# The convolution's layernorm moved behind the fifth head, its projection behind the seventh, and eight of its taps made diagonal matmuls

## The chip, the cores and the metric

One core of one Trainium2 chip runs the whole program. The metric is the device time of one execution in microseconds (us), as the median of several runs. A profile of one execution stands beside it; its times count from the start of its span.

## The reference

The program is two transformer blocks over 512 tokens of width 1024. The change lies in the mixer of the first block, where half of the width is attention and half is a gated convolution:

```python
q, k = rope(rmsnorm(q)), rope(rmsnorm(k))      # 8 heads of 64, 2 key/value heads
attn_out = softmax(q @ k.T) @ v
h = a * sigmoid(gate)                          # 512 channels
h = depthwise_conv(h, conv_dw)                 # 31 taps over time, one weight per channel and tap
h = silu(layernorm(h + conv_b))                # over the 512 channels
x = x + concat([attn_out, h]) @ w_out
```

Behind it come a product-key mixture of experts (128 candidates per token out of 16384 experts) and the whole second block (an RWKV-7 time mix, a sparse attention, a feed-forward), which the change doesn't touch.

## The kernel before

Everything is held transposed: channels on the 128 partitions, the 512 tokens along the free axis, so the 512 convolution channels are four blocks of 128x512. All of the change is in `phase1`, which fills the first 267 us. Large products are three fp32r matmuls each (`mm3`, lines 265 to 267: high by high, low by high, high by low); weights stream through `Stream.next`, which splits each 128x1024 tile on ScalarE (L246) and GpSimd (L248). Products that are given fp32 operands directly, such as the rotation of `head_norm_rope` (L381) or the channel sums (L491), appear in the trace as two matmul records per instruction.

`conv_in` makes one channel block's gated input `hp` (padded to 542 columns) and does the first five taps on ScalarE and GpSimd (`side`). `taps` is a generator: for each block it takes a PSUM bank of the tag `po`, writes tap 5 into it with one VectorE instruction (L353), adds taps 6 to 30 with one VectorE instruction each (L355, 25 of them), and adds `side` into `acc[j]` (L357). `advance(n)` draws n steps of it. Each head's `scores` writes four score tiles into the four banks of the tag `pb`, takes the row maxima (L437, L438), exponentiates into tiles `pr` (L440) and scales them on GpSimd (L442); `values` transposes them (L454, into `pb` banks), splits the result (L282, L283) and multiplies with V (L456 to L458) into a `po` bank that a pair of heads shares. `conv_norm` sums `acc` over channels (L491), squares (L497), takes the row statistics (L928, L934, L935), spreads them (L963), scales (L503), applies silu (L504) and splits (`mch`, `mcl`). `project` multiplies that by half of w_out into x (96 matmuls of 512 columns); `last` does the attention's half.

The loop over heads, with the lines around it:

```python
scores(0); advance(TAPS); conv_in()            # TAPS = 12
for s in range(8):
    if s == 0: query()
    if s < 7: scores(s + 1)
    advance(TAPS)
    values(s)
    if s == 0: conv_in()
    if s in (1, 2): query()
    if s == 3:
        advance(200)                           # all steps that are left
        cs = conv_norm()
    if s == 5:
        project(cs)
```

A planner orders the instructions: it goes through the program with estimated times, and each engine gets the earliest instruction in program order that is ready. Each engine then executes its list strictly in that order. Tiles of one tag share a fixed number of buffers (`po` 2, `mm` 2, `pb` 4, the work tiles `c2` 21, the weight tiles `c4` 12). The tiles `pr`, the splits of `values`, the squares of `conv_norm` and its eight result tiles are all `c2`.

Of the kernel before, what the change touches and what calls it, by code (L numbers as in the profile page):

```python
# [14 lines left out]
OP = mybir.AluOpType  # L15
# [3 lines left out]
P = 128  # L19
S = 512  # L20
# [201 lines left out]
class Stream:  # L222
# [30 lines left out]
    def next(self):  # L253
        self.do_split(self.i + 1 + self.ahead)
        r = self.split.pop(self.i)
        self.i += 1
        return r
# [21 lines left out]
def split_plain(c, x, name, shape=None):  # L279
    nc = c.nc  # L280
    h, lo = c.t2(name + "h", F32R), c.t2(name + "l", F32R)
    nc.scalar.copy(h, x)  # L282
    nc.vector.tensor_sub(lo, x, h)  # L283
    return h, lo
# [11 lines left out]
def phase1(c, st):  # L296
    nc = c.nc
    ident, ones, bones, rot = (c.sq[:, i, :] for i in range(4))
# [19 lines left out]
    def proj(tag="mm"):  # L318
        ps = c.bank(tag, 2)
        mm3(nc, ps, st.next(), xs, kall)  # L320
        return ps
# [3 lines left out]
    def conv_in():  # L325

        j = len(conv)
        a, g = c.t2("ca"), c.t2("cg")
        tag = "mm" if conv else "po"
        nc.vector.tensor_mul(a, proj(tag), rs)  # L330
        nc.vector.tensor_mul(g, proj(tag), rs)
        nc.scalar.activation(g, g, AF.Sigmoid)
        hp = c.sm("hp", [P, S + 30], bufs=4)
        nc.gpsimd.memset(hp[:, 0:15], 0.0)
        nc.gpsimd.memset(hp[:, S + 15:], 0.0)
        nc.vector.tensor_mul(hp[:, 15:15 + S], a, g)
        conv.append(hp)
        w, side = c.vec("cdw", j * 31, 31), c.sm("side", [P, S], bufs=4)
        nc.scalar.activation(side, hp[:, 0:S], AF.Identity, scale=w[:, 0:1], bias=c.vec("cb", j))
        for tap in range(1, SIDE):  # L340
            t = c.sm("tap", [P, S], bufs=2)
            nc.scalar.activation(t, hp[:, tap:tap + S], AF.Copy, scale=w[:, tap:tap + 1])
            nc.gpsimd.tensor_add(side, side, t)
        sides.append(side)
# [3 lines left out]
    def taps():  # L348

        for j in range(4):  # L350

            w, hp, ps = c.vec("cdw", j * 31, 31), conv[j], c.bank("po", 2)
            nc.vector.tensor_scalar(ps, hp[:, SIDE:SIDE + S], w[:, SIDE:SIDE + 1], None, op0=OP.mult)  # L353
            for tap in range(SIDE + 1, 31):
                nc.vector.scalar_tensor_tensor(ps, hp[:, tap:tap + S], w[:, tap:tap + 1], ps, op0=OP.mult, op1=OP.add)  # L355
                yield
            nc.vector.tensor_add(acc[j], ps, sides[j])  # L357
            yield

    tp = taps()  # L360

    def advance(n):
        for _ in range(n):
            next(tp, None)

    def head_norm_rope(p, g):

        t, sq = c.t2("hn"), c.t2("hsq")
        nc.scalar.activation(t, p, AF.Copy, scale=g)
        nc.scalar.activation(sq, p, AF.Square)  # L370
        pn = c.bank()
        for n in range(4):
            nc.tensor.matmul(pn[:, n * 2:n * 2 + 2], sq[:, n * P:(n + 1) * P], bones[:, 0:P:64], start=True, stop=True)
        r = c.sm("hr", [P, 4, 2], bufs=5)

        nc.vector.scalar_tensor_tensor(r, pn[:, 0:8].rearrange("p (n h) -> p n h", n=4), 1.0 / 64,
                                       e2[:, :, None].to_broadcast([P, 4, 2]), op0=OP.mult, op1=OP.add)
        rf = r.rearrange("p n h -> p (n h)")
        nc.gpsimd.tensor_tensor(rf, rf, c.mhalf, op=OP.pow)
        pr = c.bank()  # L380
        nc.tensor.matmul(pr, rot, t, start=True, stop=True)  # L381
        u = c.t2("hu")
        nc.vector.tensor_mul(u, pr, c.rope[:, 1, :])
        nc.gpsimd.tensor_mul(t, t, c.rope[:, 0, :])
        nc.vector.tensor_add(t, t, u)
        return t, r

    conv_in()
    t, r = head_norm_rope(proj(), c.vec("kg"))
    rb = c.t2("rb")  # L390
    nc.scalar.copy(rb.rearrange("p (n v) -> p n v", n=8), r.rearrange("p n h -> p (n h)")[:, :, None].to_broadcast([P, 8, 64]))
    ps = c.bank()
# [6 lines left out]
    def query():  # L399
        t, r = head_norm_rope(proj(), qg)  # L400
        qs.append(split_plain(c, t, "hs") + (r,))
# [9 lines left out]
    for kv in range(2):  # L411
        s = slice(kv * 64, kv * 64 + 64)
# [12 lines left out]
    def scores(s):  # L425
        j, kv = divmod(s, 2)
        rows = slice(kv * 64, kv * 64 + 64)
        qh, ql, r = qs[j]
        prob[s] = []
        for qi in range(4):  # L430
            sl = slice(qi * P, (qi + 1) * P)
            sc = c.bank()
            nc.tensor.matmul(sc, qh[rows, sl], kh[rows, :], start=True, stop=False)
            nc.tensor.matmul(sc, qh[rows, sl], kl[rows, :], start=False, stop=False)
            nc.tensor.matmul(sc, ql[rows, sl], kh[rows, :], start=False, stop=True)
            m, z = c.sm("mx", [P, 1]), c.sm("zs", [P, 1])
            nc.vector.tensor_reduce(m, sc, axis=AX.X, op=OP.max, negate=True)  # L437
            nc.vector.tensor_mul(m, m, r[:, qi, kv:kv + 1])  # L438
            pr = c.t2("pr")
            nc.scalar.activation(pr, sc, AF.Exp, scale=r[:, qi, kv:kv + 1], bias=m, accum_out=z)  # L440
            nc.vector.reciprocal(z, z)
            nc.gpsimd.tensor_mul(pr, pr, z.to_broadcast([P, S]))  # L442
            prob[s].append(pr)
# [22 lines left out]
    def project(xs):  # L466

        for j in range(KD):
            if j % 2 == 0:
                w = st.next()  # L470
            ps = c.bank("mm", 2)
            mm3(nc, ps, w, xs, range(4), off=j % 2 * 4)
            nc.vector.tensor_add(x[j], x[j], ps)
# [12 lines left out]
    def conv_norm():  # L486

        cv = acc
        pm = c.bank("mm", 2)
        for j in range(4):  # L490
            nc.tensor.matmul(pm, ones, cv[j], start=j == 0, stop=j == 3)  # L491

        def csquares():
            for j in range(4):
                nc.vector.scalar_tensor_tensor(cv[j], pm, -1.0 / 512, cv[j], op0=OP.mult, op1=OP.add)
                sq = c.t2("csq")
                nc.scalar.activation(sq, cv[j], AF.Square)  # L497
                yield sq

        cr = spread_rows(c, rstd_rows(c, csquares(), 1.0 / 512, EPS, 4, tag="mm"), tag="mm")  # L500
        ch, cl = [], []
        for j in range(4):
            nc.vector.tensor_mul(cv[j], cv[j], cr)  # L503
            nc.scalar.activation(cv[j], cv[j], AF.Silu, scale=c.vec("clg", j), bias=c.vec("clb", j))  # L504
            h, lo = split_plain(c, cv[j], "mc")
            ch.append(h)
            cl.append(lo)
        return ch, cl

    scores(0)  # L510
    advance(TAPS)
    conv_in()
    for s in range(8):
        if s == 0:
            query()
        if s < 7:
            scores(s + 1)
        advance(TAPS)
        values(s)
        if s == 0:  # L520
            conv_in()
        if s in (1, 2):
            query()
        if s == 3:
            advance(200)
            cs = conv_norm()
        if s == 5:
            project(cs)
    return last


HALVES = [slice(0, 256), slice(256, 512)]
SIDE = 5
TAPS = 12


# [381 lines left out]
def rstd_rows(c, sqs, scale, eps, count=KD, mean=None, tag="pb"):  # L918

    nc = c.nc
    ones = c.sq[:, 1, :]
    ps = c.bank(tag, 4 if tag == "pb" else 2)
    n = 0
    for sq in sqs:
        for i in range(4):
            nc.tensor.matmul(ps[:, i:i + 1], sq[:, i * P:(i + 1) * P], ones[:, 0:1],  # L928
                             start=n == 0 and i == 0, stop=n == count - 1 and i == 3)
        n += 1  # L930
    c.n += 1
    r = c.sb.tile([P, 4], F32, name=f"rr_{c.n}", tag="rr", bufs=4)
    mean = r if mean is None else mean
    nc.vector.tensor_scalar(mean, ps[:, 0:4], scale, eps, op0=OP.mult, op1=OP.add)  # L934
    nc.gpsimd.tensor_tensor(r, mean, c.mhalf[:, 0:4], op=OP.pow)  # L935
    return r
# [21 lines left out]
def spread_rows(c, r, dst=None, tag="pb"):  # L958

    nc = c.nc  # L960
    ps = c.bank(tag, 4 if tag == "pb" else 2)
    for i in range(4):
        nc.tensor.transpose(ps[:, i * P:(i + 1) * P], r[:, i:i + 1].to_broadcast([P, P]), c.sq[:, 0, :])  # L963
    if dst is None:
        return ps
    nc.scalar.copy(dst, ps)
    return dst
# [1157 lines left out]
```

## Time and profile before

| | us |
|---|---|
| median of 3 runs | 2903.32 |
| lowest, highest | 2900.66, 2912.34 |
| the profiled execution | 2895.1 |
| its span | 2893.3 |
| `phase1`, up to the last matmul of the heads | about 267 |

The profile lists engines as PE (TensorE matmul), PEld (its weight loads), DVE (VectorE), ACT (ScalarE), POOL (GpSimd) and SP (the queue of most DMAs). A row of the timeline is start, duration, engine, line, operation, output <- inputs, count, and in brackets the idle time before it with what ended it. Matmul records overlap: what one costs is read from the start of one to the start of the next. In a view by stretches each engine's busy time stands with its number of instructions, and then the granted TensorE clock as a share of full speed (0.50 is 1.2 GHz, 1.00 is 2.4 GHz).

### The profile page before, as it was taken

The numbers are of one execution on the slowest core, as the hardware profiler recorded it, in microseconds if no ns is written. First come the engines' busy times: TensorE is split into PE (matmuls) and PEld (weight loads), VectorE is DVE, ScalarE is ACT, GpSimd is POOL, SyncE is SP. The second block draws the span as 40 slices with busy tenths as digits, with TensorE's granted clock in tenths as the row PEclk, the third lists the DMA queues.
The fourth block names the chain that finished last, engine by engine and source line by source line (L and its number), as shares of the span: only waits on it lengthen the run. The fifth ranks groups of instructions, "written<-read, shape, count | busy, mean of one in ns | idle before, by whom it ended". The sixth has DMA issues, their size and how long they took to land.

```text
span 2893.3 us, 42190 instructions
## 1 busy us (share of the span) xinstructions
PE 2752.7 (95%) x15555; PEld 2357.6 (81%) x15555; DVE 2070.6 (72%) x3972; ACT 1222.8 (42%) x2104; POOL 1199.6 (41%) x959
## 2 busy tenths in 40 slices
PE   8959999999899999999999998999989989999998
PEld 6638899999788888888888777888877768888887
DVE  7585899988788888888885469685438865477721
ACT  5624334677333333333335542112337753444431
POOL 5713350000433333333334676433457736544444
PEclk9969999999999999999999999989989999999999
DMA  4101235688999999999975764645632236233332
GB/s 145 51 0 50 84 115 179 209 289 297 367 351 343 339 339 340 348 343 334 346 261 147 225 171 135 211 130 177 197 116 75 66 130 214 78 98 95 94 96 73
DMA packets 270915, 553.99 MB, mean 191 GB/s; under 512 B 41394, under 2 KB 147890, under 8 KB 268916
## 3 DMA queue, kind: packets, MB, share of 16 engines
q1 hardware_dynamic: 219264, 370.91, 39.7%
q0 software_dynamic: 36864, 134.23, 12.9%
q10 hardware_dynamic: 14580, 46.15, 4.4%
q8 instruction: 122, 2.00, 0.3%
q14 instruction: 85, 0.70, 0.1%
HBM read 464.77 MB, written 83.89 MB: 190 GB/s over the span
## 4 chain that ended last, share of the span: by engine, by line
PE 59%; DVE 8%; DMA 3%; POOL 2%; issue 1%; SPq 1%; ACT 0%; POOLq 0%; ACTq 0%; DVEq 0%
PE pb L858 11%; PE mm L265 8%; PE mm L267 8%; PE mm L266 8%; PE po L858 6%; PE pb L265 2%; PE pb L266 2%; PE pb L267 2%; DVE c4y L1547 1%; PE pb L1634 1%; DVE prob L1969 1%; PE pb L1646 1%; PE mm L1995 1%; DVE ptl L1998 1%; DMA kz<-nk_d 1%
## 5 line engine op out<-in xcount | busy, mean ns | idle before, releaser
L248 POOL TENSOR_TENSOR wl<-wr,wh 128x1024 fp32r<-128x1024 f32 x203 | 504.0, 2485 | 416.4 <-ACT wh L246 151.5
L246 ACT CAST wh<-wr 128x1024 fp32r<-128x1024 f32 x319 | 334.7, 1050 | 496.7 <-PE mm L266 150.6
L690 POOL DMA_INDIRECT ur<-in_u,eix x128 | 150.2, 1174 | 586.6 <-DVE og L786 182.6
L683 ACT CAST vh<-vr 128x512 fp32r<-128x512 f32 x256 | 146.0, 619 | 138.8 <-PE pb L858 138.7
L690 POOL DMA_INDIRECT vr<-in_vrow,eix x128 | 147.8, 1155 | 98.8 <-DVE acc L816 28.2
L684 DVE TENSOR_TENSOR vl<-vr,vh 128x512 fp32r<-128x512 f32 x256 | 167.2, 687 | 23.7 <-ACT vh L683 23.1
L248 DVE TENSOR_TENSOR wl<-wr,wh 128x1024 fp32r<-128x1024 f32 x116 | 142.0, 1224 | 51.6 <-ACT wh L246 50.0
L816 DVE SCALAR_TENSOR_TENSOR acc<-vr,hc,acc 128x1024 f32<-128x1024 f32 x128 | 163.6, 1278 | 0.0
L858 PE MATMUL pb<-vh,ah 128*128 128x512 f32 x512 | 159.7, 393 | 0.0
L858 PE MATMUL pb<-vl,ah 128*128 128x512 f32 x512 | 158.4, 390 | 0.0
L858 PE MATMUL pb<-vh,al 128*128 128x512 f32 x512 | 157.1, 391 | 0.0
L808 DVE CUSTOM_DVE_ANT_0 ur<-ur,hnt 128x1024 f32<-128x1024 f32 x128 | 155.6, 1218 | 0.0
L858 PEld LDWEIGHTS pb<-vl,ah 128*128 128x128 f32 x512 | 96.1, 188 | 21.9
L858 PEld LDWEIGHTS pb<-vh,ah 128*128 128x128 f32 x512 | 96.1, 188 | 20.8
L858 PEld LDWEIGHTS pb<-vh,al 128*128 128x128 f32 x512 | 96.2, 188 | 20.4
L794 ACT ACTIVATE wb<-pb 128x512 f32<-128x512 f32 x96 | 98.9, 1160 | 26.8 <-PE pb L791 25.2
L833 ACT ACTIVATE mm<-mm 128x384 f32<-128x384 f32 x60 | 28.5, 475 | 190.7 <-PE mm L267 190.7
L1976 POOL TENSOR_TENSOR prob<-prob,nz 128x128 f32<-128x128 f32 (+3 forms) x128 | 88.7, 725 | 38.5 <-DVE nz L1973 26.2
L1192 DVE TENSOR_TENSOR tot<-tot,sq 128x512 f32<-128x512 f32 x11 | 17.1, 1551 | 112.0 <-ACT sq L1189 112.0
L858 PE MATMUL po<-vh,ah 128*128 128x512 f32 x256 | 80.2, 394 | 3.2 <-ACT ah L837 3.2
L835 DVE TENSOR_TENSOR mm<-mm,wt 128x384 f32<-128x384 f32 x60 | 33.8, 564 | 67.0 <-ACT mm L833 66.8
L858 PE MATMUL po<-vh,al 128*128 128x512 f32 x256 | 79.8, 391 | 0.1
(1408 smaller groups left out, 8646.9 us busy)
## 6 DMA issues: line engine op xcount, KB each, us to landing
wr<-in_ws SPq DMA_DIRECT2D x191, 512.0 KB, 3.6
wr<-in_uT SPq DMA_DIRECT2D x128, 512.0 KB, 4.9
vr<-in_vrow SPq DMA_DIRECT2D x128, 512.0 KB, 6.7
w_d<-wb ACTq DMA_DIRECT2D x12, 2048.0 KB, 7.5
wt<-w_d SPq DMA_DIRECT2D x32, 768.0 KB, 9.4
gh_d<-gh ACTq DMA_DIRECT2D x68, 192.0 KB, 3.9
gh<-gh_d SPq DMA_DIRECT2D x68, 192.0 KB, 7.6
rd_d<-z SPq DMA_DIRECT2D x24, 256.0 KB, 3.1
```

The source lines that it names most:

```text
L246: c.nc.scalar.copy(h, r)
L248: eng.tensor_sub(lo, r, h)
L265: nc.tensor.matmul(ps, w[0][:, sl], xs[0][k], start=first and a == 0, stop=False)
L266: nc.tensor.matmul(ps, w[0][:, sl], xs[1][k], start=False, stop=False)
L267: nc.tensor.matmul(ps, w[1][:, sl], xs[0][k], start=False, stop=last and a == n - 1)
L683: nc.scalar.copy(h[:, s], r[:, s])
L684: nc.vector.tensor_sub(lo[:, s], r[:, s], h[:, s])
L690: nc.gpsimd.indirect_dma_start(out=t, out_offset=None, in_=src, in_offset=bass.IndirectOffsetOnAxis(ap=eix[:, s:s + 1], axis=0))
L794: nc.scalar.activation(wb[:, :, t4:t4 + 4].rearrange("p e t -> p t e"), wp.rearrange("p (t e) -> p t e", t=4), AF.Copy, scale=1.0 / GSCALE)
L808: nc.vector.tensor_tensor_reduce(out=u, in0=u, in1=hnt, scale=1.0, scalar=0.0, op0=OP.mult, op1=OP.add, accum_out=hc[:, s:s + 1])
L816: nc.vector.scalar_tensor_tensor(acc, v, ghs[gi][:, s:s + 1], acc, op0=OP.mult, op1=OP.add)
L858: nc.tensor.matmul(outs[i][half], ps[a][:, ts], vs[v][:, half * 512:(half + 1) * 512], start=et == 0 and n == 0, stop=et == NE - 1 and n == 2)
```

## The change

Taps 5 to 12 of each block are no longer VectorE instructions. GpSimd builds a tile `dg` of eight 128x128 diagonal matrices (the identity times the tap's weights), and eight fp32 matmuls of 512 columns accumulate these taps into the `po` bank; the whole of this is one step of the generator. VectorE goes on with taps 13 to 30. A block is thus 20 steps rather than 26. `conv_norm` is called at s == 4, behind `values(4)`, and `project` at s == 6, behind `values(6)`; `advance(200)` stays at s == 3.

```diff
-            nc.vector.tensor_scalar(ps, hp[:, SIDE:SIDE + S], w[:, SIDE:SIDE + 1], None, op0=OP.mult)
-            for tap in range(SIDE + 1, 31):
+
+            dg = c.t4("dg").rearrange("p (a b) -> p a b", a=NPE)
+            nc.gpsimd.tensor_tensor(dg, ident[:, None, :].to_broadcast([P, NPE, P]),
+                                    w[:, SIDE:SIDE + NPE, None].to_broadcast([P, NPE, P]), op=OP.mult)
+            for t in range(NPE):
+                nc.tensor.matmul(ps, dg[:, t, :], hp[:, SIDE + t:SIDE + t + S], start=t == 0, stop=t == NPE - 1)
+            yield
+            for tap in range(SIDE + NPE, 31):
                 nc.vector.scalar_tensor_tensor(ps, hp[:, tap:tap + S], w[:, tap:tap + 1], ps, op0=OP.mult, op1=OP.add)
                 yield
             nc.vector.tensor_add(acc[j], ps, sides[j])
...
         if s == 3:
             advance(200)
+        if s == 4:
             cs = conv_norm()
-        if s == 5:
+        if s == 6:
             project(cs)
...
 SIDE = 5
+NPE = 8
 TAPS = 12
```

## Rows read from the trace of the kernel before

**Rows 1.** The page, busy time, share of the span and instructions of TensorE.

```profile
PE 2752.7 (95%) x15555; PEld 2357.6 (81%) x15555; DVE 2070.6 (72%) x3972; ACT 1222.8 (42%) x2104; POOL 1199.6 (41%) x959
```

**Rows 2.** Busy times by stretches; after POOL the granted clock, DMA share, GB/s.

```profile
50.00:105.00 55.00, 53.23 (x216) 40.29 (x216) 27.69 (x53) 27.11 (x44) 38.44 (x25) 0.94 0.20 59
105.00:166.00 61.00, 55.44 (x232) 36.97 (x232) 55.70 (x114) 34.03 (x66) 32.41 (x27) 0.94 0.08 25
166.00:212.00 46.00, 12.34 (x41) 8.71 (x41) 34.63 (x55) 5.82 (x9) 1.01 (x1) 0.50 0.00 0
212.00:267.00 55.00, 54.15 (x250) 40.98 (x250) 27.17 (x57) 27.73 (x52) 21.73 (x16) 0.95 0.13 39
```

**Rows 3.** Timeline of TensorE, 165 to 222 us.

```profile
165.25 0.39 PE L435 MATMUL pb<-hsh,hsl 64*128 64x512 f32 x1
183.51 2.08 PE L491 MATMUL mm<-acc,sqm 128*128 128x512 f32 x2 [17.87 <-DVE acc L357]
195.98 2.07 PE L491 MATMUL mm<-acc,sqm 128*128 128x512 f32 x2 [10.39 <-DVE acc L357]
...
211.91 1.22 PE L265 MATMUL mm<-mch,wh 128*128 128x512 f32 x2 [2.91 <-ACT mch L282]
...
220.15 1.91 PE L454 MATMUL pb<-sqm,pr 128*128 128x128 f32 x16
```

**Rows 4.** Timeline of ScalarE, 198 to 217 us.

```profile
198.87 2.36 ACT L497 ACTIVATE csq<-acc 128x512 f32<-128x512 f32 x4 [33.50 <-DVE acc L495]
...
213.19 1.64 ACT L282 CAST mch<-acc 128x512 fp32r<-128x512 f32 x3
...
216.14 0.78 ACT L440 ACTIVATE pr<-pb,mx,hr 128x512 f32<-128x512 f32 x1
```

**Rows 5.** Timeline of VectorE, 67 to 196 us.

```profile
67.03 0.69 DVE L357 TENSOR_TENSOR acc<-po,side 128x512 f32<-128x512 f32 x1
...
108.43 0.75 DVE L353 TENSOR_SCALAR po<-hp,vecs 128x512 f32<-128x512 f32 x1
...
146.87 0.69 DVE L357 TENSOR_TENSOR acc<-po,side 128x512 f32<-128x512 f32 x1
...
168.88 0.75 DVE L353 TENSOR_SCALAR po<-hp,vecs 128x512 f32<-128x512 f32 x1
169.54 0.15 DVE L438 TENSOR_TENSOR mx<-mx,hr 128x1 f32<-128x1 f32 x1
169.60 13.26 DVE L355 SCALAR_TENSOR_TENSOR po<-hp,vecs,po 128x512 f32<-128x512 f32 x20
...
195.24 0.69 DVE L357 TENSOR_TENSOR acc<-po,side 128x512 f32<-128x512 f32 x1
```

**Rows 6.** Timeline of TensorE at 107 us: the first matmul of values(0).

```profile
107.85 0.50 PE L456 MATMUL po<-pth,avh 128*128 128x512 f32 x1
```

**Rows 7.** Groups of instructions, 25 to 267 us: busy us, mean ns, idle before.

```profile
L355 DVE SCALAR_TENSOR_TENSOR po<-hp,vecs,po 128x512 f32<-128x512 f32 x100 | 73.3, 751 | 1.2
L248 POOL TENSOR_TENSOR wl<-wr,wh 128x1024 fp32r<-128x1024 f32 x18 | 44.0, 2448 | 32.6 <-issue 15.4 <-PE mm L266 10.2 <-ACT wh L246 3.6
L442 POOL TENSOR_TENSOR pr<-pr,zs 128x512 f32<-128x512 f32 x32 | 32.6, 1043 | 38.5 <-DVE zs L441 21.9 <-DVE mx L438 16.5
```

**Rows 8.** Timeline of TensorE, 131 to 133 us: an fp32 matmul among fp32r ones.

```profile
131.44 1.10 PE L381 MATMUL pb<-hn,sqm 128*128 128x512 f32 x2
132.47 0.49 PE L433 MATMUL pb<-hsh,hsh 64*128 64x512 f32 x1
132.81 0.39 PE L434 MATMUL pb<-hsl,hsh 64*128 64x512 f32 x1
133.04 0.39 PE L435 MATMUL pb<-hsh,hsl 64*128 64x512 f32 x1
```

**Rows 9.** Timelines of VectorE and GpSimd at 45 us, side by side.

```profile
45.27 1.28 POOL L343 TENSOR_TENSOR side<-side,tap 128x512 f32<-128x512 f32 x1
45.35 1.75 DVE L385 TENSOR_TENSOR hn<-hn,hu 128x512 f32<-128x512 f32 x1
```

## The prediction, made before the change was run

> **What bounds the kernel now.** The first view is the page's busy table: TensorE is busy for 95% of the span [rows 1], so time can be gained only where it waits, or lost by giving it work. The second is the busy time by stretches [rows 2]. In `phase1` TensorE is full from 50 to 105 us (53.23 of 55), nearly so from 105 to 166 (55.44 of 61) and from 212 to 267 (54.15 of 55), but from 166 to 212 it is busy for 12.34 of 46, at a granted clock of 0.50; there VectorE is busiest, with 34.63. The timeline of TensorE says for what it waits [rows 3]: after the last score matmul at 165.25 it stands idle for 17.87 and then 10.39 us, each time for an `acc` (L357), which is the end of a block's taps. VectorE's timeline shows these taps running with little between them from 168.88 to 195.24 [rows 5].
>
> The third question is why the heads stop meanwhile. The maxima of head 5 were done at 169.54 [rows 5], yet its first exponential ran at 216.14, behind `csq` at 198.87 and `mch` at 213.19 [rows 4]; ScalarE had been idle 33.50 us. All of these take `c2` tiles, and their order is the program's (`conv_norm` stands ahead of scores(5)). I read it as buffers of one tag being handed out in program order. The `po` banks say the same: block 0 was complete at 67.03, but block 1 began at 108.43, right behind the first matmul of values(0) at 107.85, whose bank comes before it in the program [rows 5, 6].
>
> **The moved norm.** With `conv_norm` behind values(4), head 5's exponentials and head 4's values no longer stand behind it. They fill the wait with the transposes (1.91 us [rows 3]), 12 matmuls of 512 columns at 0.23 (start to start [rows 8]), 2.8, and the twelve of scores(6), 2.8: 7.5 us of TensorE that now run behind 212. Head 6's exponentials then stand behind `mch` as head 5's did, so TensorE runs dry again after these. `project` is filler in either place, 96 matmuls of 0.23 or 22 us; one step later it competes less with values(5) and scores(7), and I cost that at nothing as the stretch from 212 on is full. Its weights stay in `c4` one step longer, and `last`'s are loaded behind them; GpSimd and ScalarE are half idle there [rows 2], and if that cover failed a weight tile's split would cost 2.45 [rows 7].
>
> **The taps on TensorE.** VectorE loses 32 instructions: 0.663 each where they run in a row (13.26 over 20 [rows 5]), 0.751 as the mean of records [rows 7], so 21 to 24 us. Block 0's quarter of it ran beside a full TensorE and is worth nothing.
>
> TensorE gains 32 fp32 matmuls of 512 columns. The fp32 matmul of L381 starts at 131.44 and the next one at 132.47 [rows 8], 1.03 us; the next record is 0.10 longer than its like, so at least 0.93 is the engine's own. I take 0.95, near the row, 30 us in sum. The bounds: 0.46, if two records followed each other as fp32r ones do (15 us in all), and 1.04 (2.08 at half clock halved [rows 3], 33 us); a block's eight at half clock would be 16.6 rather than 7.6.
>
> GpSimd builds `dg` four times, 1024 columns each: 2.1 from the scaling by a broadcast factor (2 x 1.043) to 2.45 from the subtraction of two full tiles [rows 7], 8 to 10 us in all, on an engine that is half idle. On the path lies only the last one, and only if it is built late; I take 0, at most 2.5. Its `c4` buffer is one of 12 for the time of eight matmuls; I take that as free, since the weights are split two tiles ahead, and bound it by one split, 2.45.
>
> An addition of two SBUF tiles on VectorE took 1.75 us beside GpSimd's at 45.27 [rows 9], while one with a PSUM operand takes 0.69 [rows 5]: up to 1.1 lost for a collision. The Trainium skill (SBUF — State Buffer, section SBUF: two separate sides) has a rule for this that speaks against the new GpSimd work: VectorE with two SBUF inputs and GpSimd hold their common port pair for a whole instruction, and the other blocks. By it four more tiles cost VectorE up to 10 us, by the row 4.4; the taps read PSUM and one SBUF tile and would escape, so neither changes my sum by more than a microsecond.
>
> **The sum, from place to place.** Blocks 0 and 1 need only their gated inputs and, being 20 steps long, both stand ahead of values(0) now. Their 16 matmuls (15.2) meet a TensorE with 1.8 idle in 55 us and push everything by 15. VectorE, 27.69 busy of 55 there, takes their other taps at no cost. Blocks 2 and 3 (15.2) fall into what was 105 to 166, where 5.6 us are idle; I let them fill 4, and push by 11. So the scores of head 5 end near 165.6 + 15 + 11 = 192.
>
> Block 3 needs a `po` bank, which it gets when block 2 is complete and values(2) has begun. Counting block 2's matmuls to about 160 and its 18 taps among the heads' work to about 175, block 3's matmuls share TensorE with values(3) and end near 187. Then 18 taps at 0.66 to 0.75 and some 3 us of head 4's subtractions give the last `acc` at about 202. From the end of the last `acc` (195.93) to the first matmul of `project` (211.91) took 16.0 [rows 3, 5]; some of it at half clock, so 13 to 16 now, and `project` starts at 216. Of the 55 us behind it (212 to 267), 7.5 have moved ahead and some 2.5 of half-clock matmuls at its start are kept as they are: 47.5, and `phase1` ends at 263 to 264 rather than 267. That is 3 to 4 us; a count by TensorE alone gives the frame: before, 33.7 idle in 166 to 212, 6 lost to the clock there and 7.4 idle in 50 to 166, 47 in all; after, 30 more work, 10 to 12 idle at the norm's chain, some 2 lost to the clock and 2 to 4 idle before it, 44 to 48: between -1 and 3. I take 4, because VectorE, at 55.70 of 61 before, no longer delays the heads' steps, which neither count includes. The rest of the program depends on x and is TensorE-bound, so that it moves by the same.
>
> The profiled execution took 2895.1 (span 2893.3 and 1.8 around it), 8.2 below the median of 2903.3. It would become 2891, and the median 2899.
>
> **The rivals.** *The wait vanishes altogether* (faster): the planner places block 3's matmuls before values(3), so that the last `acc` is there when the heads are, near 190. For it speaks VectorE's freed 21 us; against it that block 3 needs block 2's bank. The gain is 47 - 30 = 17, and with matmuls of 0.85 20: 2883 to 2886. Chance 0.2.
>
> *The diagonal matmuls come last* (slower): block 3's eight go behind scores(5), as the planner prefers earlier program lines and TensorE has a backlog of 26 us by then. Place: between the last `acc` and the first `mch` matmul. 192 + 7.6 + 18 x 0.75 + 3 + 16 = 232, and 47.5 behind it: 279.5, 12 us later, 2916. It decides from a last `acc` later than about 204 (204 + 16 + 47.5 = 267.5). For it speaks that TensorE has no room from 50 to 166; against it the latency gaps in values(3), which something must fill. Chance 0.22.
>
> *The move does nothing*: head 5's exponentials still come behind `csq`, for a reason other than the tag's order. Then 7.5 us stay behind the chain, and `phase1` ends near 271, 2907. Against it speaks each order seen in rows 4 to 6. Chance 0.05, and the forecast has 0.53.
>
> **The numbers.** My forecast's own range is a gain of -2 to 11, 2892 to 2905. A measurement of this kernel tells about 0.5% (14.5 us) from no change, so the forecast counts as the same, as does half of the first rival, nearly all of the third, and two thirds of the second. Faster by over 0.5%: 0.16; slower: 0.07; the same: 0.77. The range for 8 in 10 is 2883 to 2913, which takes in the first rival's upper half and most of the second.
>
> **What would show it.** Of after: 64 records of diagonal matmuls, 0.9 to 1.05 us per pair; 72 taps at L355's form; block 1's taps ahead of the first L456 rather than behind it; head 5's exponentials ahead of `csq`; an idle time of TensorE of 10 to 12 us ending at `csq`, the statistics or `mch`; the last `acc` near 202 and the end of the heads near 263. It is wrong if the last `acc` is before 193 or behind 208, if the diagonal matmuls cost under 0.8 or over 1.2, or if a later stage moves by more than the first.

## The result, and the profile after

The changed kernel takes 2919.05 us (median of 11 executions, 2903.53 to 2938.09) beside 2904.09 for the kernel before: a ratio of 1.0053, 95% interval 1.0037 to 1.0070. It is slower by some 15 us, where 2899 and "the same" were forecast. Its profiled execution took 2928.19, in the upper half of its times; that of the kernel before took 2895.1, below the lowest of its 11 (2896.96), so the two profiles lie further apart than the medians.

The first view is the one of [rows 2], of the kernel after: busy times by stretches, the granted clock behind POOL.

```profile
50.00:105.00 55.00, 54.41 (x213) 37.46 (x213) 37.14 (x60) 24.17 (x40) 41.29 (x27) 1.00 0.18 58
105.00:166.00 61.00, 57.25 (x237) 38.39 (x237) 46.99 (x90) 31.21 (x56) 34.50 (x25) 0.97 0.11 35
166.00:212.00 46.00, 37.52 (x139) 22.38 (x138) 31.00 (x65) 16.52 (x32) 9.17 (x9) 0.85 0.00 1
212.00:267.00 55.00, 50.90 (x250) 40.44 (x251) 26.53 (x52) 25.58 (x46) 17.60 (x12) 0.91 0.13 41
```

The hole from 166 to 212 is closed: TensorE is busy for 37.52 us of it instead of 12.34, at 0.85 instead of 0.50. TensorE's timeline, beside [rows 3]: block 1's diagonal matmuls, the last of block 3's, the last wait for `acc`, the norm's chain, the first matmul of `project`, the first of the attention's own projection (`last`).

```profile
89.24 7.03 PE L358 MATMUL po<-hp,dg 128*128 128x512 f32 x16
...
172.68 1.99 PE L358 MATMUL po<-hp,dg 128*128 128x512 f32 x4
...
200.05 2.07 PE L497 MATMUL mm<-acc,sqm 128*128 128x512 f32 x2 [3.83 <-DVE acc L363]
203.57 6.99 PE L936 MATMUL mm<-sqm,csq 128*128 128x1 f32 x32 [1.45 <-ACT csq L503]
211.89 1.12 PE L971 MATMUL mm<-sqm,rr 128*128 128x128 f32 x4 [1.34 <-POOL rr L943]
215.92 1.22 PE L265 MATMUL mm<-mch,wh 128*128 128x512 f32 x2 [2.91 <-ACT mch L282]
...
261.70 0.50 PE L265 MATMUL mm<-mxh,wh 128*128 128x256 f32 x2 [0.67 <-ACT mxh L467]
```

ScalarE's timeline, beside [rows 4]: head 5's exponentials now come ahead of `csq`.

```profile
184.29 0.78 ACT L446 ACTIVATE pr<-pb,mx,hr 128x512 f32<-128x512 f32 x1
...
202.88 2.48 ACT L503 ACTIVATE csq<-acc 128x512 f32<-128x512 f32 x4 [12.94 <-DVE acc L501]
```

VectorE's timeline, beside [rows 5]: the first tap of block 3 and the last `acc`.

```profile
174.70 0.76 DVE L361 SCALAR_TENSOR_TENSOR po<-hp,vecs,po 128x512 f32<-128x512 f32 x1 [1.03 <-PE po L358]
...
199.30 0.69 DVE L363 TENSOR_TENSOR acc<-po,side 128x512 f32<-128x512 f32 x1
```

The changed groups, beside [rows 7] (25 to 267 us): the taps left on VectorE, the matmuls, the building of `dg`.

```profile
L361 DVE SCALAR_TENSOR_TENSOR po<-hp,vecs,po 128x512 f32<-128x512 f32 x72 | 54.0, 750 | 15.8 <-PE po L358 15.2
L358 PE MATMUL po<-hp,dg 128*128 128x512 f32 x64 | 29.2, 598 | 0.6 <-POOL dg L355 0.6
...
L355 POOL TENSOR_TENSOR dg<-sqm,vecs 128x1024 f32<-128x1024 f32 x4 | 7.6, 1902 | 0.1
```

`last` begins at 261.70; in the kernel before the same matmul stands at 267.05. Phase 1 is 5.35 us shorter, and yet the program is longer. Where the time goes is seen when both spans are cut at the same work: the end of phase 1, the end of the experts, the last VectorE product of the second block's inverses (`invert`, L1547 in the numbering of before), the last store of its RWKV scan (`chunks`, L1748), the end. Some matmuls of `invert` still run inside what is called the scan here. Kernel before:

```profile
0.00:267.00 267.00, 211.19 (x892) 155.22 (x892) 176.30 (x319) 123.46 (x207) 124.50 (x94) 0.87 0.19 61
267.00:1534.00 1267.00, 1251.10 (x6987) 1127.21 (x6988) 1062.25 (x2195) 538.22 (x860) 369.35 (x288) 1.00 0.80 280
1534.00:1925.00 391.00, 371.59 (x2317) 305.13 (x2317) 282.33 (x394) 144.61 (x230) 221.63 (x155) 0.95 0.59 176
1925.00:2161.00 236.00, 224.39 (x1855) 193.69 (x1853) 108.58 (x235) 62.80 (x110) 102.10 (x85) 0.95 0.56 167
2161.00:2893.00 732.00, 694.38 (x3506) 576.30 (x3506) 441.15 (x833) 353.69 (x697) 382.01 (x338) 0.98 0.32 101
```

The changed kernel:

```profile
0.00:262.00 262.00, 233.54 (x958) 163.69 (x958) 162.28 (x288) 123.03 (x207) 131.65 (x98) 0.94 0.19 63
262.00:1525.00 1263.00, 1248.91 (x6988) 1124.50 (x6986) 1060.00 (x2195) 535.12 (x860) 382.59 (x288) 1.00 0.80 281
1525.00:1921.00 396.00, 376.02 (x2315) 308.75 (x2316) 283.48 (x392) 144.23 (x229) 218.34 (x154) 0.94 0.56 172
1921.00:2194.00 273.00, 256.49 (x1857) 224.55 (x1856) 109.86 (x236) 63.15 (x111) 103.68 (x85) 0.81 0.49 148
2194.00:2926.00 732.00, 695.85 (x3506) 577.58 (x3506) 435.95 (x833) 354.14 (x697) 382.37 (x338) 0.97 0.32 101
```

The fourth rows hold most of it: the same scan, some 1855 matmul records, none of them touched by the change, takes 273 us instead of 236 (the third rows lose 5 more). The granted clock says how: 236 x 0.95 = 224 and 273 x 0.81 = 221. By this estimate both would take about the same at full clock, and the 37 us are what longer stretches at 1.2 GHz cost. In pieces, the changed kernel's scan:

```profile
1925.00:1953.00 28.00, 27.50 (x164) 24.56 (x164) 18.42 (x44) 1.50 (x3) 7.09 (x12) 0.51 0.51 133
...
1960.00:1972.00 12.00, 11.78 (x153) 10.85 (x153) 5.69 (x11) 2.58 (x5) 4.53 (x11) 1.00 0.37 132
...
1973.00:2003.00 30.00, 30.00 (x309) 27.71 (x308) 14.05 (x30) 1.52 (x3) 3.58 (x3) 0.50 0.29 90
...
2026.00:2043.00 17.00, 14.80 (x66) 13.50 (x67) 4.72 (x11) 4.30 (x8) 11.24 (x9) 0.60 0.62 192
...
2130.00:2160.00 30.00, 26.56 (x121) 24.73 (x121) 8.59 (x19) 7.23 (x15) 7.49 (x6) 0.55 0.30 93
```

and the kernel before's, where the falls of 1973 and 2026 have no counterpart and the other two are shorter:

```profile
1930.00:1942.00 12.00, 11.99 (x64) 11.43 (x65) 4.58 (x13) 1.50 (x3) 4.47 (x8) 0.57 0.47 89
1942.00:2105.00 163.00, 160.45 (x1492) 137.10 (x1492) 81.17 (x183) 40.93 (x71) 66.47 (x58) 1.00 0.61 186
2105.00:2118.00 13.00, 10.81 (x55) 9.91 (x55) 2.40 (x5) 5.09 (x10) 5.29 (x4) 0.64 0.44 143
```

TensorE's timeline of the changed kernel has these waits there; the kernel before has none at the places of the second and the third:

```profile
1925.49 0.69 PE L1654 MATMUL pb<-tokv,A 128*128 128x64 f32 x2 [1.87 <-DVE A L1645]
...
1960.22 0.63 PE L1629 MATMUL pb<-sqm,ck 128*128 128x128 f32 x4 [1.92 <-DMA ck<-rd_d]
...
2028.20 0.47 PE L1751 MATMUL pb<-sqm,Y 128*128 128x128 f32 x1 [4.26 <-ACT o L1752]
```

The third stands right ahead of its fall. The second ended at 1960, and the clock stayed at 1.00 for 12 us behind it before it fell at 1973: that this wait let it fall is not shown, and e9 takes it up.

The two programs differ there in one thing, the order. The planner weaves 31 side projections (24 matmuls of 512 columns each) into the scan's small matmuls (32 to 128 columns). Of the second block's 6387 TensorE instructions 962 stand at another place in the changed kernel's list. The longest row of scan matmuls, those of `invert` counted in, without a projection or key matmul in between is 76 before and 288 after; in the changed kernel's profile it stands from 1957 to 2006, and the fall of 1973 to 2003 lies inside it.

**Theory A**: phase 1 gained about what was forecast, and the planner's other order in the second block lost more. **Rival B**: something that the new first stages leave behind slows TensorE, whatever the order. A second rival: one of the two edits costs the time by itself.

### The profile page after: what moved, and what is told of

Same layout as the page of the kernel before. It is cut to its first block, busy times and chain, and to the rows that moved or that the text cites. A ratio compares the mean times of both kernels' runs of the same rounds, so it can differ in the third digit from the quotient of the medians.

```text
span 2926.4 us, 42282 instructions
## 1 busy us (share of the span) xinstructions
PE 2810.8 (96%) x15619; PEld 2399.1 (82%) x15619; DVE 2051.6 (70%) x3940; ACT 1219.7 (42%) x2104; POOL 1218.6 (42%) x963
## 4 chain that ended last, share of the span: by engine, by line
PE 60%; DVE 8%; DMA 3%; POOL 1%; issue 1%; ACT 1%; SPq 1%; POOLq 0%; ACTq 0%; DVEq 0%
PE pb L866 11%; PE mm L266 8%; PE mm L267 8%; PE mm L265 8%; PE po L866 6%; PE pb L265 2%; PE pb L266 2%; PE pb L267 2%; DVE c4y L1555 1%; PE pb L1642 1%; PE pb L1654 1%; PE mm L2003 1%; DVE prob L1977 1%; DMA wr<-in_uT 1%; DVE c4y L1545 1%
## 5 line engine op out<-in xcount | busy, mean ns | idle before, releaser
L698 POOL DMA_INDIRECT vr<-in_vrow,eix x128 | 158.1, 1235 | 77.2 <-issue 25.2
```

Of the source, the lines that this page charges most:

```text
L698: nc.gpsimd.indirect_dma_start(out=t, out_offset=None, in_=src, in_offset=bass.IndirectOffsetOnAxis(ap=eix[:, s:s + 1], axis=0))
```

## The experiments

Each ratio is to the kernel before on the same chip, with its 95% interval.

**The order fixed (e1, e2).** The second block's program is instruction for instruction the same in both kernels, so the list of one can be imposed on the other by edges that fix only the order of issue:

```diff
+            was = {id(i) for i in tc.nc.cur_bb.bb.instructions}
             block2(c, st2, px)
+            fixed_order(tc, [i for i in tc.nc.cur_bb.bb.instructions if id(i) not in was])
...
+def fixed_order(tc, traced):
+    for engine, runs in ORDER.items():          # ORDER: the other kernel's list, here of TensorE
+        own = [i for i in traced if str(i.engine).endswith("." + engine) and "PoolBoundary" not in type(i).__name__]
+        order = [own[k] for s, n in runs for k in range(s, s + n)]
...
+        for a, b in zip(order, order[1:]):
+            tc.add_manual_dep(b, a.name, mybir.DependencyInfo(mybir.DependencyClass.NoSync, mybir.DependencyReason.DATA),
+                              reason="fixed_order")
```

> The changed kernel (both parts of the change), with TensorE's instruction order in the second block (everything from the group norm of block 2 on, 6387 matmuls) fixed by order-only edges to the order that it had in the kernel before; nothing else is edited. The planner had put 962 of these 6387 at other places in the changed kernel. Theory A (phase 1 gains as forecast, and the loss is the other interleaving of the second block's scan with its side projections, which the planner chose): the scan's loss goes and phase 1's gain stays. The keys' last matmul of L1820 ends near 2047 us instead of 2076 (before: 2054), time 2904 less 4 to 9 = 2895 to 2900, ratio 0.997 to 0.9985 to the kernel before. Rival B (TensorE is slowed in the scan by something that the changed first stages leave behind, whatever the order): 2919, ratio 1.005, L1820 near 2076. Rival C (half and half): 2905 to 2912.

Measured: 2900.68, ratio 0.9992 (0.9979 to 1.0005); L1820's last matmul starts at 2053.1, against 2054.4 in the kernel before. The loss is gone; of the gain of 4 to 9 us only about 2 remain, which the interval does not tell from none.

> The kernel before, unchanged in phase 1, with TensorE's instruction order in the second block fixed to the one that the changed kernel has. Theory A: it takes over the changed kernel's loss without its gain: 2919 plus 4 to 9 = 2923 to 2928, ratio 1.0065 to 1.0085; up to 2939 if all of the 42 us that the profiled execution lost between 1925 and 2195 us come back. Rival B: 2904, ratio 1.000. Rival C: 2910 to 2916.

Measured: 2930.50, ratio 1.0086 (1.0065 to 1.0107). A kernel in which phase 1 is untouched becomes slower by 25 us through TensorE's order alone. Theory A stands, B falls.

**The two edits apart (e3, e4)**, with the old TensorE order:

```diff
+        if s == 4:
             cs = conv_norm()
-        if s == 5:
+        if s == 6:
             project(cs)
```

is e3, from the kernel before; e4 undoes just these lines in the changed kernel.

> The kernel before with the moved norm and projection alone (norm behind the fifth head's values, projection behind the seventh's scores), all taps on VectorE, and TensorE's order in the second block fixed to that of the kernel before. By the prediction's steps: the last tap stays near 196, 7.5 us of TensorE's work (transposes, values of head 4, scores of head 6) come ahead of the projection, phase 1 ends near 259.5 instead of 267: 2904 - 7.5 = 2897, ratio 0.9975. Rival B (the move brings the loss): 2919. Rival: the move does nothing, 2904, ratio 1.000.

Measured: 2910.19, ratio 1.0018 (1.0003 to 1.0032).

> The kernel before with eight taps of each block as diagonal matmuls alone, norm and projection at their old places, TensorE's order in the second block fixed to that of the kernel before. By the prediction's steps: 30 us more on TensorE, the scores of head 5 end near 192 and the last tap near 202, then the chain of 13 to 16 and the 55 us behind it: phase 1 ends near 271 to 273 instead of 267, time 2904 + 5 = 2909, ratio 1.0015. Rival B (the taps bring the loss): 2919 or more, ratio 1.005. Rival: VectorE's relief wins 5 us or more, 2899.

Measured: 2914.59, ratio 1.0032 (1.0019 to 1.0045). Both come out later than expected, e3 by 13 us and e4 by 6. In both profiles the last addition of phase 1's projection starts earlier than before (294.1 and 291.5 against 296.1), and the scan is longer again, with waits of 10.4 and 9.9 us for VectorE's A from 1870 to 2000, against 5.6 in the kernel before. TensorE's list was fixed, VectorE's was not; e6 and e7 try that.

**All five engines fixed (e5 to e8)**: the same edges, with `ORDER` holding the lists of TensorE, VectorE, ScalarE, GpSimd and SyncE.

> The changed kernel with the order of all five engines in the second block (TensorE, VectorE, ScalarE, GpSimd and SyncE's transfers) fixed to that of the kernel before. With TensorE's order alone (e1) one wait of 6.9 us on VectorE's A (L1645) was left, which the kernel before has with 3.0 there, and 8 of the 10 us that the kernel was ahead at the end of the inverse (1914.6 against 1924.9) were given back by the end of L1582. Theory A (the orders decide): what is ahead at the end of the inverse, 4 to 10 us, arrives at the end: 2894 to 2899, ratio 0.9965 to 0.9985. Rival (a stage that is reached some us earlier loses the gain to the clock in any order): 2901 to 2905, ratio 0.999 to 1.0005.

Measured: 2893.91, ratio 0.9971 (0.9957 to 0.9984). The change is worth 8 us where the second block's order is the old one.

> The moved norm and projection alone, with the order of all five engines in the second block as in the kernel before. In e3 the last matmul of the attention's projection ended 2.0 us earlier than before (294.1 against 296.1) and the peer's sums 1.3 earlier, but the scan lost 17 with waits of 10.4 us on VectorE's A. Theory A: the scan's loss goes, 2902, ratio 0.9993 (0.9985 to 1.000). Rival (the move itself costs the time that e3 showed): 2910, ratio 1.002.

Measured: 2900.74, ratio 0.9990 (0.9973 to 1.0007): as Theory A said, no loss left.

> The diagonal taps alone, norm and projection at their old places, with the order of all five engines in the second block as in the kernel before. In e4 the last matmul of the attention's projection ended 4.6 us earlier than before (291.5 against 296.1) and the peer's sums 6.5 earlier, but the scan lost 22. Theory A: the scan's loss goes, 2897 to 2899, ratio 0.998 (0.997 to 0.999). Rival (the taps themselves cost the time that e4 showed): 2914, ratio 1.003.

Measured: 2897.97, ratio 0.9986 (0.9970 to 1.0003): as Theory A said. Neither edit costs anything by itself.

> The kernel before with the order of all five engines in the second block fixed to that of the changed kernel. Theory A: the loss that the changed kernel shows between the end of the inverse and the end of the scan's last L1748 (273 us in its profile against 236 before) comes back: 2904 + 20 to 37 = 2924 to 2941, ratio 1.007 to 1.013. Rival (TensorE's order alone carried it all, as in e2): 2930, ratio 1.0086 (within it). Rival (no effect of the order by itself): 2904, ratio 1.000.

Measured: 2930.65, ratio 1.0113 (1.0092 to 1.0135): as Theory A said. By the ratio the order costs 33 us here (27 to 39 by the interval), by the medians 28, and in e2, with TensorE's order alone, 25. Less the change's gain of 8 that leaves 17 to 25, and the changed kernel shows 15 (11 to 20): the order carries the loss, and a remainder of up to 10 us is not clear of noise.

**What in the order costs it (e9, e10, e13, e14).** Extra matmuls (`matmul(ps, xg0h[:, :128], xg0h)`, overwritten by the real ones) are put into the waits:

```diff
+        WARM.append((at, [c.nc.tensor.matmul(ps, c.warm[:, :P], c.warm, start=True, stop=True).ins for _ in range(count)]))
```

> As e8 (the kernel before, second block in the changed kernel's order), with only the two waits filled that this order has and the old one has not: nine extra matmuls of 512 columns, whose result is overwritten, ahead of the L1621 that waited 1.93 us for ck, and nine projection matmuls put ahead of the L1743 that waited 2.08 us (they stood behind it). In e8's profile the granted clock was half for some 20 us behind the first and some 12 us behind the second. Theory A2 (the loss is the half clock that follows these two waits): it falls by half of 32, and by part of the waits: 16 to 20 us, 2911 to 2915, ratio 1.0045 to 1.006. Rival (the 288 small matmuls of the scan that stand in a row without a projection are slow by themselves): 2931 to 2934, ratio 1.011 to 1.0125.

Measured: 2923.35, ratio 1.0069 (1.0052 to 1.0085). Some 7 us came back by the medians and 13 by the ratios (e8 and e9 ran on two chips), where 16 to 20 were expected, and the clock fell where the theory had no wait for it. The view by stretches of e9:

```profile
1966.00:1978.00 12.00, 12.00 (x167) 10.98 (x166) 5.32 (x9) 2.45 (x5) 4.19 (x10) 1.00 0.37 133
1978.00:1992.00 14.00, 14.00 (x197) 12.57 (x196) 8.71 (x21) 1.04 (x2) 2.53 (x2) 0.51 0.25 69
```

TensorE was busy without a gap from 1966 on, as far as the profile's records tell, with matmuls of 32 to 128 columns, and the clock fell at 1978 all the same. (The other wait was not shortened by the moved projections: TensorE stood idle for 2.90 us ahead of 2023, where it was 2.08 in e8.)

> As e5 (the changed kernel, second block in the old order), with 36 extra matmuls of 512 columns, whose results are overwritten, twelve (2.7 us) each ahead of three waits: the two for VectorE's A (L1654, 2.63 and 2.98 us in e5) and the L1751 that waited 3.26 us for tokv. It adds only work. Theory A2 (each such wait is followed by TensorE at half clock; in e5's profile for some 6, 24 and 30 us): the clock stays up, half of the 60 us comes back: 15 to 30 us, 2864 to 2879, ratio 0.987 to 0.992. Rival (the extra matmuls cost nothing and win nothing, the clock falls anyway): 2894 to 2898, ratio 0.997 to 0.9985. Rival (they delay what waits): up to 8 us slower, 2902.

Measured: 2880.98, ratio 0.9929 (0.9913 to 0.9945): 36 matmuls of pure extra work make the kernel 13 us faster than e5, just under the 15 to 30 expected (the two ran on different chips; by the ratios it is 12). Two waits of e5, its second for A and the one for tokv, and the stretches behind them:

```profile
1923.45 0.69 PE L1654 MATMUL pb<-tokv,A 128*128 128x64 f32 x2 [2.98 <-DVE A L1645]
...
2109.44 0.45 PE L1751 MATMUL pb<-sqm,Y 128*128 128x128 f32 x1 [3.26 <-ACT tokv L1631]
```

```profile
1922.00:1948.00 26.00, 24.55 (x143) 23.09 (x144) 16.84 (x44) 2.09 (x4) 5.77 (x10) 0.50 0.45 112
...
2107.00:2138.00 31.00, 28.56 (x125) 26.57 (x126) 8.87 (x20) 7.42 (x16) 8.46 (x6) 0.56 0.25 79
```

and e10 over the same work, with one short fall (behind another wait, 1.98 us for GpSimd's Y) left:

```profile
1916.00:1923.00 7.00, 7.00 (x29) 5.99 (x29) 6.01 (x5) 0.92 (x2) 1.88 (x1) 0.56 0.81 264
1923.00:2141.00 218.00, 215.26 (x1846) 185.06 (x1844) 101.33 (x228) 57.99 (x102) 97.59 (x82) 1.00 0.55 166
```

This is the fastest version of all; e5, e11 and e14 also beat both kernels, by less.

> As e9 (the kernel before, second block in the changed kernel's order, nine extra matmuls ahead of the L1621 that waited for ck), and besides: six extra matmuls of 512 columns at each of three places inside the 288 small ones (18 in all, 18 x 0.23 = 4 us of pure extra work where TensorE does not wait), and twelve ahead of the L1743 that still waited 2.90 us in e9, in place of the moved projections. In e9 the granted clock fell near 1978 us although TensorE had been busy without a gap since 1966, with matmuls of 32 to 128 columns. Theory A3 (a row of small matmuls lets the clock fall as an idle wait does, and matmuls of 512 columns among them keep it): no fall between 1960 and 2000, and none behind the second wait: 14 and 13 us at half clock come back by half, the wait of 2.9 goes, 4 are added: 2923 - 7 - 6.5 - 3 + 4 = 2910, 2906 to 2914, ratio 1.001 to 1.004. Rival A2 (only idle waits let it fall, the fall in e9 came from the earlier wait at 1925 to 1930): the fall inside the row stays, 2918 to 2921, ratio 1.005 to 1.006. Rival (extra matmuls cost and win nothing): 2927, ratio 1.008.

Measured: 2921.02, ratio 1.0071 (1.0047 to 1.0096): the clock did what A3 said, the time did not. The stretches of e13 that answer to e9's:

```profile
1966.00:1978.00 12.00, 12.00 (x132) 10.69 (x131) 5.57 (x10) 1.99 (x4) 4.96 (x11) 1.00 0.22 75
1978.00:1992.00 14.00, 14.00 (x266) 11.87 (x264) 8.05 (x21) 2.09 (x4) 2.56 (x2) 1.00 0.35 111
```

No fall from 1960 to 2050. But e13 has 30 extra matmuls more than e9 (7 us at 0.23), a new wait of 1.98 us stood ahead of L1830, and the fall behind an untouched wait at 2127 lasted 24 us where e9's lasted 10. All four profiles with the new order and no filler in the row (the changed kernel's, e2's, e8's, e9's) have a fall inside the row, and e13's has none. So the clock fell in the row of small matmuls without a wait, as far as one profile with fillers can show; extra work in the row paid for itself and no more.

> The kernel before, unchanged in phase 1 and in its order, with the same 36 extra matmuls ahead of the same three waits as in e10. What e10 won over e5 (2894 to 2881, 13 us) would come without the change too: 2890, ratio 0.9955 (0.994 to 0.997). e10 beside it is then the change alone in a second block that keeps its clock: by the forecast 4 us, by e5 against the kernel before 8 to 9 us, 0.9985 to 0.997 of this kernel. Rival (the fillers work only with the changed kernel's timing): 2903, ratio 1.000.

Measured: 2895.16, ratio 0.9974 (0.9958 to 0.9990): the fillers work without the change, for 8 us where 13 were expected. In its profile the clock still fell for some 20 us, 5 us behind the third filled place, where the longest idle time was 0.59 us:

```profile
2108.00:2129.00 21.00, 21.00 (x91) 19.51 (x91) 8.34 (x20) 3.43 (x9) 3.59 (x3) 0.51 0.22 61
```

e10 is 14 us below it (2880.98 to 2895.16, on two chips), against the 8 of e5: the change is worth 8 to 14 us.

**A planner's remedy, and a third draw (e11, e12).**

```diff
+            tc.strict_bb_all_engine_barrier()
             block2(c, st2, px)
```

> The changed kernel with one barrier of all engines ahead of the second block, and no order fixed by hand. With it the planner by itself gives the second block nearly the old order (the longest row of scan matmuls without a projection or key matmul is 76, as in the kernel before, and 288 in the changed kernel). Theory A: e5's gain, less what the barrier costs at the seam, which no run has shown: between 0 and 8 us, so 2894 to 2902, ratio 0.997 to 1.000. Rival (the barrier costs as much as the order wins): 2919, 1.0055.

Measured: 2893.88, ratio 0.9971 (0.9958 to 0.9984): e5's gain without any list fixed by hand. The ratio is that of the whole, so a cost of the barrier, if there is one, is in it.

> The diagonal taps alone, with the order that the planner chose for them: a third order of the scan (longest row without a projection or key matmul 154, against 76 before and 288 in the changed kernel). Theory A: e7's gain of 4 us, less a loss between those of the two other orders (0 and 28 us): 2905 to 2920, ratio 1.001 to 1.006. Rival (only the changed kernel's order is bad): 2898, ratio 0.9985.

Measured: 2903.48, ratio 1.0008 (0.9994 to 1.0022): 6 us more than e7 and just under what Theory A gave, for an order whose longest row (154) lies between the two others. The intervals of e12 and e7 touch, and the scan takes 245 and 242 us in the two profiles, so that a loss by this third order is not shown.

## Why the prediction was wrong

The step that failed is the last one of the sum: "The rest of the program depends on x and is TensorE-bound, so that it moves by the same." Every instruction behind phase 1 was held to stay in its place and only to start earlier. The planner made a new list for the whole program, also where nothing was edited; that the planner works with estimated times stands in the section on the kernel before, and the prediction did not follow it past 267 us. The scan then took 37 us more in the profiles, and the order alone costs 25 us in e2 and 33 in e8. "TensorE-bound" hid the second half of the error: a busy TensorE [rows 1] is not one at full clock, and in these runs the clock of the same matmuls changed with their order. The scan over all 16 profiles, from the last L1547 to the last L1748 as above:

| kernel | us | mean clock | product |
|---|---|---|---|
| before | 236 | 0.95 | 224 |
| after | 273 | 0.81 | 221 |
| e2, new TensorE order | 257 | 0.86 | 221 |
| e8, new order of all | 261 | 0.84 | 219 |
| e5, old order of all | 252 | 0.88 | 222 |
| e11, barrier | 244 | 0.91 | 222 |
| e14, before, filled | 241 | 0.93 | 224 |
| e10, after, filled | 230 | 0.98 | 225 |
| the eight others | 242 to 260 | 0.87 to 0.94 | 219 to 233 |

The work is 219 to 225 us at full clock in the eight that are named; what differs is the clock (e1, e3, e4 and e13, at 229 to 233, also hold the waits or the extra work told above). e5 has the order of before and 252 us in its profile, its slowest execution: the length of a fall varies by itself. The wait for A was 2.95 us before and 2.98 in e5, and the clock stayed low for 12 and for 26 us. So the 37 us are in part luck of the two profiles; the medians say 15 and the 8 that the change is worth.

All executions say the same of the clock, not only the profiled ones. The changed kernel's spans have a mean of 2918.9 us at a granted clock of 0.9646, e5's 2892.9 at 0.9728: length times clock is 2816 and 2814. The kernel before on e5's chip has 2900.4 at 0.9658, e8 2930.8 at 0.9553: 2801 and 2800. Where only the order of the second block differs, the work at full clock is the same and the clock is the whole difference.

The prediction itself named "if a later stage moves by more than the first" as what would make it wrong. It was given no chance and no price. (The chances for the whole do not follow from the list either: half of the first rival's 0.2 is 0.10 for faster, not 0.16, and 0.83 are left for the same.)

Point by point, what concerned phase 1 held:
- *The end of phase 1*: 263 to 264 forecast, 261.70 measured, 5.35 us earlier against "3 to 4"; neither rival that wins or loses by the wait (17 to 20 us earlier, 12 later) is it.
- *The moved norm*: head 5's exponentials come ahead of `csq`, as read from [rows 4]. Start of `project` 216 forecast, 215.92 measured; from the end of the last `acc` to it 15.9 us, within 13 to 16. Of the 10 to 12 us idle named for the norm's chain, 5.7 are there at `csq`, `rr` and `mch`, and 3.8 more stand ahead of them at the last `acc`.
- *The last `acc`*: 202 forecast; its instruction starts at 199.30. The scores of head 5 ended at 184.7 rather than 192: TensorE was pushed by 19 us and not by 26. Block 3's matmuls ended at 174.7 where 187 was counted, and its 18 taps, among the heads' maxima and splits, took 24.6 us where 15 to 16.5 were counted. The two errors nearly cancel, so that the last `acc`, and with it the start of `project`, came out so near is luck in part.
- *The diagonal matmuls*: 0.95 us taken, eight in 7.03, 0.88 each, just under the 0.9 to 1.05 named; 32 of them 29.2 us against 30. `dg` took 1.90 against 2.1 to 2.45, 7.6 us in all, and TensorE waited 0.6 us for it. One of the four met an addition of VectorE, which took 2.37 us, against 1.75 in [rows 9]: the collision is there and worth less than a microsecond, as was taken.
- *Blocks 0 and 1 ahead of values(0)*: block 1's matmuls stand at 89.24, the first matmul of values at 114.6. Held.

How the two edits share the gain, as the mean of the profiles with the same phase 1:

| | profiles | last addition of phase 1's projection | last of the experts' sums |
|---|---|---|---|
| as before | 6 | 297.0 | 1535.1 |
| the move alone | 2 | 294.5 | 1530.5 |
| the taps alone | 3 | 293.1 | 1529.9 |
| both | 5 | 289.7 | 1522.8 |

The move wins 2.5, the taps 3.9, both 7.3. The same phase 1 differs from profile to profile (293.5 to 299.9 in the six as before), so the two single gains are rough; with both, 288.2 to 290.8, the gain is clear. The expectation that the taps alone would lose 5 (e4) and the move alone win 7.5 (e3) finds no support here. The experts win another 5 beside; the planner's list differs there as well, and this was not tried apart.

Two things stay open: what in the planner's estimates turned the scan's order (with a barrier ahead of the block the longest row is 76 again, which fits with what runs on from the earlier stages, but no run took the planner's times apart), and how the order's price divides between the long row and the waits that came with it, as the runs that filled them also shifted the falls elsewhere.

## What to carry to other kernels

Where a planner orders the program, an edit draws a new order for every stage behind it: compare the lists far from the edit before its time is put down to the edit, and separate the two by fixing the order or by a barrier at the seam (some 25 us lost and 8 won looked like one loss of 15). A forecast of a few microseconds needs a range as wide as such a draw. And a busy share says nothing of the clock: length times granted clock is a quick estimate of whether a stage has more work or runs slower.

## What the runs showed of the hardware

- TensorE's clock fell to 0.50 (1.2 GHz) at idle times of 1.87 and 4.26 us in the changed kernel and of 2.98 and 3.26 in e5, and stayed there for 7 us (e10) to 28 (changed kernel) although TensorE was busy for most of it (24.55 of 26 us at 0.50 in e5). It did not fall right behind every such idle time: it stayed at 1.00 for 12 us behind the one of 1.92. The Trainium skill (TensorE: Matmul & The Clock Gate, section A second HAM failure mode: psum-queue depth-cycling) reports of a bf16 kernel with matmuls of 512 columns that short idles between groups of matmuls made the clock swing between its two levels and cost throughput; the traces here agree, in a scan whose own matmuls are fp32 and have 32 to 128 columns.
- It fell without an idle time in the profile too, in a row of matmuls of 32 to 128 columns (e9, 1978 us), and did not in the one profile where 18 matmuls of 512 columns stood among them (e13).
- Useless work can pay: 36 matmuls in three waits won 12 to 13 us with the change (e5 to e10) and 8 without it (e14).
